# Work moved off GpSimd in an RWKV-7 mixer, a branch moved inside a layer of experts, and two weight loads swapped

## The chip, the cores and the metric

The kernel runs on one core of a Trainium2 chip. The metric is the device time of one execution, in microseconds (us). TensorE (PE) does the matrix products; VectorE (DVE), ScalarE (ACT) and GpSimd (POOL) do the element-wise work; SyncE (SP) issues nearly all DMA transfers. Each engine takes its own instructions in order and waits on semaphores for the others.

## The reference

256 tokens of width 1024, all in float32, pass through a first block (two layers of retention and block attention, not touched here) and a second block of two layers. Each layer of the second block is a mixer followed by a two-level mixture of 32 experts. The two mixers, cut to what matters:

```python
def even_mixer(h, ...):                    # layer 0
    u = h @ w_in
    m = u_rw + (token_shift(u_rw) - u_rw) * mu
    r, k, v, dw, da, dg = split(m)
    decay = exp(-exp(-softplus(-(w0 + tanh(dw) @ w2)) - 0.5))
    a = sigmoid(a0 + da @ a2);  g = sigmoid(dg) @ g2
    kk = heads(k * k_k)
    kk = kk / max(sqrt(sum(kk * kk, -1)), 1e-12)      # the norm of kk
    k = k * (1 + (a - 1) * k_a)
    y = rwkv7_recurrence(r, decay, k, v, -kk, kk * a) # S = S(diag w + a b^T) + v k^T ; y = S r
    bonus = sum(r * k * r_k, -1) * v
    o_rw = (groupnorm(y) * ln_g + ln_b + bonus) * g
    return concat([o_rw, multiscale_pool(u_pool)]) @ w_out

def odd_mixer(h, ...):                     # layer 1
    q, k, v, u_s5 = split(h @ w_in)
    o_attn = differential attention over q, k, v
    y = Re(C states) + D u_s5              # S5: one complex diagonal state per group
    z = gelu(y);  o_ssm = z * sigmoid(z @ w_glu)
    return concat([o_attn, o_ssm]) @ w_out
```

The experts (`hier_moe`) pick one of eight groups for a token and two of its four experts, and each expert is `down(silu(gate(x)) * up(x))`.

## The kernel before

**Weights.** A float32 product is made of three faster ones: the weight is split into a rounded part `hi` (a copy on ACT) and the rest `lo` (a subtraction, named `wlo`). Weights stand in a ring of SBUF slots `w0`, `w1`, ... `load_w` takes the next slot of a written-out order (`self.order`) and issues the load on SP's queue. The load waits there until the slot's last reader is done, and everything behind it in the queue waits as well.

**Even mixer** (`rwkv`, lines 1160 to 1530). The projections are made in pieces of 128 columns by `shifted` (PE at L1208 to L1210, 24 matmuls a piece from `hi` and `lo`), evacuated by DVE at L1213 and mixed with the token before by ACT at L1214 and DVE at L1215. The `lo` parts of the twelve pieces of k, r and v (four each, in this order) come from POOL at L1076; those of the pooling branch behind them come from DVE at L328. Then the decay's running sum (L1254), the norm of kk (an inverse square root by Newton's method, the chain `kkn` at L265 to L272 on tiles of 128x16, transposed by PE at L1280, spread by PE at L1289 and multiplied in at L1290), and block-diagonal operands `bbd`, `kbd`, `vbd` of two heads each (64 rows of one, 64 of the other). The recurrence is then solved in chunks of 64 tokens: products inside a chunk (L1403) and between chunks (L1411 to L1413), a small triangular inverse on DVE (L1421 to L1446, result `Tn`), and block products on PE (L1502). `LabO` and `LkO` hold the between-chunk products in block-diagonal form; DVE writes them at L1451 and L1482 as the PSUM tile times a 0/1 mask "bd". `P1` and `P2` are the gate and bonus of the output, made on POOL at L1334 to L1342.

**Experts** (`moe`). Eight groups of four experts, `for e0 in range(0, 32, 4)`. Each expert takes three matrices of 2 MB through the ring. An expert that more than 32 tokens chose is finished by `overflow`, a loop inside `tc.If(nblk > 0)`; with these inputs the branch (L1005) isn't taken, but every engine still passes it. It stands ahead of the last group, e0 = 28.

**Odd mixer** (`odd_heads`). SP's loads in their order: the matrices of q, k and S5's u, then `Tt`, S5's Toeplitz table (eight transfers at L1866 that read rows of 128 float32 from a DRAM scratch `s5H`), then v's matrix, the first half of `odd_w_out`, `s5_glu`, the second half. `Tt` is first read by the matmuls at L2041, v's matrix by the projection `ev`.

A scheduler sorts each engine's instructions by priority and by its own estimate of when they can start; `self.after(x)` puts what is issued inside it behind instruction x.

Of the kernel before, what the change touches and what calls it, by code (L numbers as in the profile page):

```python
# [19 lines left out]
T = 256  # L20
# [65 lines left out]
def even_consts():  # L86
    c = Packer()
    q = np.arange(128)
    h, s = q // 64, q % 64
    t = np.arange(64)  # L90
    same = lambda a, b, n: (a[:, None] // n) == (b[None, :] // n)
    lt = s[:, None] < t[None, :]
    both = lambda m: np.stack([m * (h[:, None] == g) for g in range(2)], axis=1)
    c.add("m16", lt & same(s, t, 16))
    c.add("incl", s[:, None] <= t[None, :])
    c.add("mo1", both(lt & same(s, t, 32) & ~same(s, t, 16)))
    c.add("mo2", both(lt & ~same(s, t, 32)))
    c.add("strict", both(lt))
    c.add("bd", both(np.ones((128, 64))))
    c.add("eye16", np.tile(np.eye(16).reshape(1, 256), (128, 1)))  # L100
    c.add("half", np.stack([q % 2 == 0, q % 2 == 1], axis=1))
    c.add("centre", (h[:, None] == h[None, :]) * (np.eye(128) - 1.0 / 64))
    sel = np.zeros((128, 4, 8))
    for p in range(4):
        sel[q, p, 2 * p + h] = 1.0
    c.add("sel", sel)
    selT = np.zeros((128, 4, 128))
    selT[:8] = sel.transpose(2, 1, 0)
    pm = np.zeros((128, 4, 3, 128))
# [37 lines left out]
class K:  # L147
# [112 lines left out]
    def rsqrt(self, sm, v, n, name, scratch=None):  # L260
        nc = self.nc
        if scratch is None:
            scratch = [sm.tile([128, n], F32, name=name + c) for c in ("_y", "_a", "_h")]
        y, a, h = scratch
        nc.vector.tensor_scalar(y.bitcast(I32), v.bitcast(I32), -0.5, float(0x5f3759df),  # L265
                                op0=ALU.mult, op1=ALU.add)
        for _ in range(2):
            nc.vector.tensor_mul(a, y, y)
            nc.vector.tensor_mul(h, a, v)
            nc.vector.tensor_scalar(a, h, 0.375, -1.25, op0=ALU.mult, op1=ALU.add)  # L270
            nc.vector.tensor_mul(a, a, h)
            nc.vector.scalar_tensor_tensor(y, a, 1.875, y, op0=ALU.add, op1=ALU.mult)  # L272
        return y
# [606 lines left out]
    def moe(self, l):  # L880
# [6 lines left out]
        with ctx:  # L887
# [11 lines left out]
            for e0 in range(0, 32, 4):  # L899
                last = e0 == 28  # L900
                if l == 0 and e0 == 8:
                    self.side = self.s5_prep()
                if e0 == 28:
                    if l == 0:
                        self.tick(99)
                    self.overflow(l, R, wk, pool, acc)
# [240 lines left out]
    def rwkv(self, keep):  # L1147
# [54 lines left out]
        def shifted(w, c, i, dst):  # L1202

            ps = X([128, T])
            wh, wl = w[c] if type(w) is list else self.wsplit(w, c, last_lo if i in (4, 5) and i not in (4, 5, 6, 7, 0, 1, 2, 3, 8, 9, 10, 11) else None,
                                                             nc.gpsimd if i in (4, 5, 6, 7, 0, 1, 2, 3, 8, 9, 10, 11) else None)
            for k in range(8):
# [54 lines left out]
        lam = Eg[:, :, 64:65].rearrange("p (a b) o -> p a (b o)", a=4)  # L1262
        for src, dst in ((0, 0), (1, 3), (2, 5)):
            nc.vector.tensor_copy(E6[:, :, dst], lam[:, :, src])
        nc.vector.tensor_mul(E6[:, :, 1], lam[:, :, 0], lam[:, :, 1])
        nc.vector.tensor_mul(E6[:, :, 4], lam[:, :, 1], lam[:, :, 2])
        nc.vector.tensor_mul(E6[:, :, 2], E6[:, :, 1], lam[:, :, 2])

# [3 lines left out]
        for p in range(4):  # L1272
            shifted(wr_, p, p, r[:, p])
        sv = prep.tile([128, 16], F32, name="kkv")
        for t in range(2):
            nc.vector.tensor_scalar(sv[:, 8 * t:8 * t + 8], ss[t], 1e-24, None, op0=ALU.max)
        rs_ = self.rsqrt(prep, sv, 16, "kkn")
        q = W([8, T])
        for t in range(2):
            nc.tensor.transpose(q[:, t * 128:(t + 1) * 128], rs_[:, 8 * t:8 * t + 8], self.ident)  # L1280
        rs = prep.tile([128, T], F32, name="kkr")[0:8]
        nc.vector.tensor_copy(rs, q)
        hka = prep.tile([128, 2, 4], F32, name="hka")
# [9 lines left out]
        u16 = lambda x: x.rearrange("p a (b t) -> p (a b) t", t=64)  # L1293
        nc.vector.tensor_mul(k, k, f)
        ar = AR0.rearrange("p a b x t -> p (a b) x t")
        nc.vector.scalar_tensor_tensor(ar[:, :, 0], u16(kk), -1.0, Eg[:, :, 0:64], op0=ALU.mult, op1=ALU.mult)
        nc.vector.tensor_scalar(ta, ta, 0.5, 0.5, op0=ALU.mult, op1=ALU.add)
        nc.vector.tensor_mul(kk, kk, ta)
        for h in range(2):
            hs = slice(64 * h, 64 * h + 64)  # L1300
            nc.vector.tensor_mul(bbd[hs, :, h], u16(kk)[hs], Ei[hs])
            nc.gpsimd.tensor_mul(kbd[hs, :, h], u16(k)[hs], Ei[hs])


        nc.vector.tensor_mul(ar[:, :, 1], u16(r), Eg[:, :, 1:65])

        rk = sq
        nc.gpsimd.tensor_mul(rk, r, k)
        srk = prep.tile([128, 32], F32, name="srk")
# [4 lines left out]
        for t in range(2):  # L1314
# [7 lines left out]
        wv_ = load(2)
        v = prep.tile([128, 4, T], F32, name="v", tag="tk")
        for p in range(4):
            shifted(wv_, p, 8 + p, v[:, p])
        for h in range(2):
            hs = slice(64 * h, 64 * h + 64)
            nc.scalar.activation(vbd[hs, :, h], u16(v)[hs], AF.Copy)
        for t in range(2):
# [3 lines left out]
            nc.scalar.activation(g, q, AF.Copy)  # L1333
            nc.gpsimd.tensor_mul(P1[:, t], g, lngb[:, 0])  # L1334
            q = W([128, 4, 128])
            for p in range(4):
# [3 lines left out]
                                 bon[:, t][:, :, None].to_broadcast([128, 8, 64]))  # L1340
            nc.gpsimd.tensor_add(P2[:, t], P2[:, t], lngb[:, 1])
            nc.gpsimd.tensor_mul(P2[:, t], P2[:, t], g)  # L1342

# [104 lines left out]
        for p in range(4):  # L1448
            qa, qb = offd(p, bbd, X if p in (0, 1, 2, 3) else W)
            for j, q in enumerate((qa, qb)):  # L1450
                nc.vector.tensor_mul(LabO[:, p, 3 * j:3 * j + 3], b4(q[:, :, 0:64], 3), mk("bd", 3))  # L1451
            cp = lambda o, n, x: nc.scalar.activation(
# [16 lines left out]
        for p in range(4):  # L1469
# [11 lines left out]
            for j, q in enumerate((qa, qb)):  # L1481
                nc.vector.tensor_mul(LkO[:, 3 * j:3 * j + 3], b4(q[:, :, 0:64], 3), mk("bd", 3))  # L1482
            cp = lambda o, n, x: nc.scalar.activation(
# [357 lines left out]
    def odd_heads(self, sm, pa, m, ctx):  # L1841
# [4 lines left out]
        load = lambda b, **kw: self.load_w(A["odd_in"][b], (8, 512), **kw)  # L1846
        self.order = [0, 4, 0, 4, 0, 2, 4, 3]
        wq = load(0, parts=2)
# [12 lines left out]
        wk_, wu = load(1), load(3)  # L1861
        Vt, Wt = (S[n_].rearrange("p (g x) -> p g x", g=32) for n_ in ("V", "W"))
        Tt = self.load_slot()
        for k in range(8):
            src = bass.AP(tensor=S["H"].tensor, offset=S["H"].offset + 16 * k, ap=[[240, 16], [32 * 240, 32], [1, 128]])
            nc.sync.dma_start(Tt[16 * k:16 * k + 16].rearrange("p (g x) -> p g x", g=32), src)  # L1866
        Tt = Tt.rearrange("p (g x) -> p g x", g=32)
        wv = load(2)
        wo0 = self.load_w(A["odd_w_out"][0], (8, 512))
        wgl = self.load_w(A["s5_glu"], (4, 512))  # L1870
        wo1 = self.load_w(A["odd_w_out"][1], (8, 512))
# [403 lines left out]
```

## Time and profile before

| | |
|---|---|
| median of 3 runs | 1618.96 us (1616.09 to 1620.35) |
| the profiled execution | 1615.62 us, of which the span of its instructions is 1613.6 us |
| PE busy | 1304.4 us (81%), mean granted clock 0.91 |
| DVE, ACT, POOL busy | 629.3, 406.5, 256.0 us |
| DMA | 499.22 MB, 309 GB/s in the mean |

By place in the trace: the first block ends at about 345 us, the even mixer at 565, the first layer of experts at 1017, the odd mixer at 1165, and the second layer of experts runs to the end. Busy times are to be read with care: PE's is the sum of its matmuls at whatever clock it was granted, so a stretch at half clock shows more of it for the same work.

### The profile page before, as it was taken

The page shows a single profiled execution, that of the slowest core. Times are in us where ns is not written, and L with a number is a line of the kernel's source. Part 1 is how long each engine was busy: PE and PEld are TensorE (multiplying, and loading weights), DVE is VectorE, ACT ScalarE, POOL GpSimd, SP SyncE. Part 2 cuts the span into 40 slices and gives each one's busy share as a digit, 9 for nine tenths or more (in the row PEclk, how much of TensorE's full clock was granted, in tenths as well). Part 3 has the DMA queues.
Part 4 walks back from the last instruction along what each step waited for, and adds up shares of the span by engine and source line. Part 5 has one row for each costly group of instructions (what it writes and reads, how often), then busy time and mean ns, then how long its engine had stood idle before and what let it go on. Part 6 is the DMA issues. An engine that isn't in the chain of part 4 may idle for free. (4 is left out here: it accounts for less than half of the span.)

```text
span 1613.6 us, 31866 instructions
## 1 busy us (share of the span) xinstructions
PE 1304.4 (81%) x13994; PEld 959.8 (59%) x13994; DVE 629.3 (39%) x1460; ACT 406.5 (25%) x759; POOL 256.0 (16%) x322
## 2 busy tenths in 40 slices
PE   7999999986989788678686658877888677777767
PEld 6887788785879665535544425656765533443434
DVE  7687678768583611511111001738611111010011
ACT  5455545554332200001110001525300000000001
POOL 2200020045323100271452000202300000000000
PEclk9999999997899799779898979987999988898879
DMA  9554344332242889999999999558799999999996
GB/s 352 196 190 157 128 185 179 133 147 105 95 157 101 317 361 425 402 426 425 420 419 422 424 381 416 158 94 326 297 425 425 424 426 426 426 426 426 424 423 287
DMA packets 51368, 499.22 MB, mean 309 GB/s; under 512 B 9452, under 2 KB 16784, under 8 KB 20632
## 3 DMA queue, kind: packets, MB, share of 16 engines
q1 hardware_dynamic: 50648, 492.40, 75.9%
q0 software_dynamic: 288, 4.19, 0.7%
q8 instruction: 113, 1.85, 0.5%
q10 hardware_dynamic: 288, 0.52, 0.1%
q14 instruction: 31, 0.25, 0.0%
HBM read 495.06 MB, written 2.04 MB: 308 GB/s over the span
## 5 line engine op out<-in xcount | busy, mean ns | idle before, releaser
L856 PE MATMUL mm<-w,xt 128*32 128x128 f32 x8192 | 300.3, 299 | 109.1 <-DMA w<-in_moe_w_up_dram 41.3
L856 PEld LDWEIGHTS mm<-w,xt 128*32 128x32 f32 x8192 | 254.2, 120 | 150.8 <-issue 89.2
L936 PE MATMUL mm<-w,hidT 128*32 128x512 f32 x896 | 189.8, 667 | 53.0 <-DMA w<-in_moe_w_down_dram 52.9
L328 DVE TENSOR_TENSOR wlo<-w,whi 128x1024 fp32r<-128x1024 f32 x116 | 143.1, 1239 | 55.3 <-ACT whi L327 54.5
L327 ACT ACTIVATE whi<-w 128x1024 fp32r<-128x1024 f32 x124 | 130.7, 1058 | 130.9 <-PE pj L338 89.0
L860 DVE SCALAR_TENSOR_TENSOR hid<-hid,mm 128x128 f32<-128x128 f32 x64 | 18.3, 286 | 371.5 <-ACT hid L859 371.5
L936 PEld LDWEIGHTS mm<-w,hidT 128*32 128x32 f32 x896 | 43.2, 118 | 166.2 <-issue 121.7
L336 PE MATMUL pj<-whi,hT 128*128 128x512 f32 x316 | 123.4, 404 | 19.1 <-ACT whi L327 17.5
L337 PE MATMUL pj<-wlo,hT 128*128 128x512 f32 x316 | 126.0, 403 | 0.0
L338 PE MATMUL pj<-whi,hT 128*128 128x512 f32 x316 | 122.9, 397 | 0.7 <-DVE hT L308 0.7
L870 DVE SCALAR_TENSOR_TENSOR y<-mm,slotsc,y 128x512 fp32r<-128x512 f32 x36 | 26.9, 750 | 190.2 <-ACT y L869 187.5
L845 PEld LDWEIGHTS tp<-ohs,x 128*128 128x128 f32 x512 | 73.8, 232 | 30.2 <-issue 25.1
L845 PE MATMUL tp<-ohs,x 128*128 128x128 f32 x512 | 77.2, 319 | 17.9 <-DVE ohs L797 17.4
L869 ACT ACTIVATE y<-mm,slotsc 128x512 fp32r<-128x512 f32 x36 | 24.7, 687 | 261.5 <-PE mm L936 239.5
L859 ACT ACTIVATE hid<-mm 128x128 f32<-128x128 f32 x64 | 17.7, 277 | 271.8 <-PE mm L856 271.8
L336 PEld LDWEIGHTS pj<-whi,hT 128*128 128x128 f32 x316 | 60.3, 192 | 32.6 <-ACT whi L327 17.7
L337 PEld LDWEIGHTS pj<-wlo,hT 128*128 128x128 f32 x316 | 60.3, 191 | 13.8 <-DVE wlo L328 1.4
L338 PEld LDWEIGHTS pj<-whi,hT 128*128 128x128 f32 x316 | 60.0, 190 | 13.3 <-DVE hT L308 1.1
L877 PE MATMUL acc<-y,ohT 128*128 128x512 f32 x144 | 49.4, 444 | 12.3 <-ACT y L869 6.2
L846 DVE TENSOR_TENSOR xt<-tp,pk 128x512 f32<-128x512 f32 x32 | 22.1, 691 | 91.0 <-PE tp L845 91.0
L864 ACT ACTIVATE hidT<-tp 128x128 f32<-128x128 f32 x64 | 17.7, 277 | 142.4 <-PE tp L863 142.4
L877 PEld LDWEIGHTS acc<-y,ohT 128*128 128x128 f32 x144 | 23.2, 193 | 42.2 <-issue 17.1
(728 smaller groups left out, 2128.3 us busy)
## 6 DMA issues: line engine op xcount, KB each, us to landing
w<-in_moe_w_gate_dram SPq DMA_DIRECT2D x64, 2048.0 KB, 30.1
w<-in_moe_w_up_dram SPq DMA_DIRECT2D x64, 2048.0 KB, 21.1
w<-in_moe_w_down_dram SPq DMA_DIRECT2D x54, 2048.0 KB, 28.8
w<-in_w_in_dram SPq DMA_DIRECT2D x14, 2048.0 KB, 7.7
w<-in_moe_w_down_dram SPq DMA_DIRECT2D x16, 1024.0 KB, 15.8
w<-in_w_out_dram SPq DMA_DIRECT2D x4, 2048.0 KB, 7.8
w<-in_w_ple_gate_dram SPq DMA_DIRECT2D x4, 2048.0 KB, 7.6
w<-in_even_in_dram SPq DMA_DIRECT2D x4, 2048.0 KB, 7.8
```

The source lines that it names most:

```text
L327: nc.scalar.activation(h, w[:, i:i + s], AF.Copy)
L328: (engine or nc.vector).tensor_sub(l, w[:, i:i + s], h.bitcast(F32))
L336: nc.tensor.matmul(out, ah, wh, start=start, stop=False)
L337: nc.tensor.matmul(out, ah, wl, start=False, stop=False)
L338: return nc.tensor.matmul(out, al, wh, start=False, stop=stop)
L845: nc.tensor.matmul(p[:, k], xk[t][:, 4 * h + k], ohs[:, t], start=t == 0, stop=t == 1)
L846: nc.vector.tensor_mul(xt[:, ks], p, R["g"][:, ks, None].to_broadcast([128, 4, 128]))
L856: nc.tensor.matmul(gu[32 * q:32 * q + 32, i], xt(k), w[:, k, 128 * q:128 * q + 128], start=k == 0, stop=k == 7)
L869: nc.scalar.activation(y[0][b][r], dn[r], AF.Copy, scale=sc[r, 0:1])
L870: nc.vector.scalar_tensor_tensor(y[1][b][r], dn[r], sc[r, 0:1], y[0][b][r].bitcast(F32), op0=ALU.mult, op1=ALU.subtract)
L877: self.nc.tensor.matmul(acc[t][b], ohT[r, t], y[i][b][r], start=start and i == 0, stop=stop and i == 1)
L936: nc.tensor.matmul(dn[32 * j:32 * j + 32], hT[j][:, k], wd[j][:, 4 * b + k], start=k == 0, stop=k == 3)
```

## The change

In the even mixer the twelve `lo` subtractions of L1076, `kbd`, `rk` (tile `sq`), `P1` and `P2` move from POOL to DVE, so that no element-wise product of the projections is left on POOL; the kkn chain gets a higher priority and some products are put behind it with `after`; v's load and projection come ahead of the bonus. The masks of `LabO` and `LkO` become a zero fill on POOL and two half-tile copies on ACT (`heads`). The overflow branch moves from e0 = 28 to e0 = 16. In the odd mixer v's matrix is loaded ahead of `Tt`, into `Tt`'s old slot 4 (`Tt` takes slot 0, v's old one), and `s5_glu` ahead of the first half of `odd_w_out`.

```diff
-                if e0 == 28:
-                    if l == 0:
-                        self.tick(99)
+                if l == 0 and last:
+                    self.tick(99)
+                if e0 == 16:
                     self.overflow(l, R, wk, pool, acc)
...
-    def wsplit(self, w, c, behind=None, engine=None):
+    def wsplit(self, w, c):
...
-        with self.after(behind) if behind else ExitStack():
-            (engine or nc.vector).tensor_sub(wl, wc, wh.bitcast(F32))
+        nc.vector.tensor_sub(wl, wc, wh.bitcast(F32))
...
+        with self.tc.high_priority(offset=300):
+            sv = prep.tile([128, 16], F32, name="kkv")
+            for t in range(2):
+                nc.vector.tensor_scalar(sv[:, 8 * t:8 * t + 8], ss[t], 1e-24, None, op0=ALU.max)
+            rs_ = self.rsqrt(prep, sv, 16, "kkn")
+            kkn = self.last_rs
...
+        with self.after(kkn):
+            for src, dst in ((0, 0), (1, 3), (2, 5)):
+                nc.vector.tensor_copy(E6[:, :, dst], lam[:, :, src])
...
-            nc.gpsimd.tensor_mul(kbd[hs, :, h], u16(k)[hs], Ei[hs])
+            with self.after(kkr):
+                nc.vector.tensor_mul(kbd[hs, :, h], u16(k)[hs], Ei[hs])
...
+        wv_ = load(2)
+        v = prep.tile([128, 4, T], F32, name="v", tag="tk")
+        for p in range(4):
+            with self.after(kkr):
+                shifted(wv_, p, 8 + p, v[:, p])
+
         rk = sq
-        nc.gpsimd.tensor_mul(rk, r, k)
+        nc.vector.tensor_mul(rk, r, k)
...
-            nc.gpsimd.tensor_mul(P1[:, t], g, lngb[:, 0])
+            nc.vector.tensor_mul(P1[:, t], q, lngb[:, 0])
...
-            nc.gpsimd.tensor_add(P2[:, t], P2[:, t], lngb[:, 1])
-            nc.gpsimd.tensor_mul(P2[:, t], P2[:, t], g)
+            nc.vector.tensor_add(P2[:, t], P2[:, t], lngb[:, 1])
+            nc.vector.tensor_mul(P2[:, t], P2[:, t], g)
...
+        for z in (LabO, *LkOs):
+            nc.gpsimd.memset(z, 0.0)
+
+        def heads(dst, q):
+
+            for h in range(2):
+                hs = slice(64 * h, 64 * h + 64)
+                nc.scalar.activation(dst[hs, :, h], q[hs, :, 0:64], AF.Copy)
...
-                nc.vector.tensor_mul(LabO[:, p, 3 * j:3 * j + 3], b4(q[:, :, 0:64], 3), mk("bd", 3))
+                heads(LabO[:, p, 3 * j:3 * j + 3], q)
...
-        self.order = [0, 4, 0, 4, 0, 2, 4, 3]
+        self.order = [0, 4, 0, 4, 0, 4, 2, 3]
...
+        wv = load(2)
         Tt = self.load_slot()
...
-        wv = load(2)
+        wgl = self.load_w(A["s5_glu"], (4, 512))
         wo0 = self.load_w(A["odd_w_out"][0], (8, 512))
-        wgl = self.load_w(A["s5_glu"], (4, 512))
         wo1 = self.load_w(A["odd_w_out"][1], (8, 512))
```

How this changes an engine's order is shown at three places. First DVE in the even mixer, around the kkn chain (`kkn_y`, `kkn_a`, `kkn_h` are its tiles, `kkv` its input; `up`, `r` the evacuation and mixing of a piece of r). Before:

```order
L265 TENSOR_SCALAR kkn_y<-kkv 128x16
L1264 COPY E_2924<-Eg 128x4 x3
L1265 TENSOR_TENSOR E_2924<-Eg 128x4
L1266 TENSOR_TENSOR E_2924<-Eg 128x4
L268 TENSOR_TENSOR kkn_a<-kkn_y 128x16
L1215 SCALAR_TENSOR_TENSOR r<-up_3015,evc,r 128x256
L1267 TENSOR_TENSOR E_2924<-E_2924,Eg 128x4
L1294 TENSOR_TENSOR k<-k,sq 128x1024
L269 TENSOR_TENSOR kkn_h<-kkn_a,kkv 128x16
L1297 TENSOR_SCALAR ta<-ta 128x1024
L1213 TENSOR_TENSOR up_3016<-x,rstdb 128x256
L270 TENSOR_SCALAR kkn_a<-kkn_h 128x16
```

After:

```order
L264 TENSOR_SCALAR kkn_y<-kkv 128x16
L1212 SCALAR_TENSOR_TENSOR r<-up_3015,evc,r 128x256
L267 TENSOR_TENSOR kkn_a<-kkn_y 128x16
L268 TENSOR_TENSOR kkn_h<-kkn_a,kkv 128x16
L269 TENSOR_SCALAR kkn_a<-kkn_h 128x16
L1210 TENSOR_TENSOR up_3016<-x,rstdb 128x256
L270 TENSOR_TENSOR kkn_a<-kkn_a,kkn_h 128x16
L271 SCALAR_TENSOR_TENSOR kkn_y<-kkn_a,kkn_y 128x16
L267 TENSOR_TENSOR kkn_a<-kkn_y 128x16
L268 TENSOR_TENSOR kkn_h<-kkn_a,kkv 128x16
L269 TENSOR_SCALAR kkn_a<-kkn_h 128x16
L1212 SCALAR_TENSOR_TENSOR r<-up_3016,evc,r 128x256
```

The products of `E`, k and ta (`L1264` to `L1267`, `L1294`, `L1297`) no longer stand inside the chain; only the evacuations of r do.

Second POOL in the same mixer, from its first work on the projections on. Before:

```order
L1076 TENSOR_TENSOR wlo<-w_2939,whi 128x1024 x2
L1165 MEMSET bbd 128x2048
L1165 MEMSET kbd 128x2048
L1165 MEMSET vbd 128x2048
L679 MEMSET pk 128x2x4
L1176 COPY sel<-evc 128x32
L1076 TENSOR_TENSOR wlo<-w_2939,whi 128x1024 x2
L1076 TENSOR_TENSOR wlo<-w_3274,whi 128x1024 x4
L1076 TENSOR_TENSOR wlo<-w_3474,whi 128x1024
L1302 TENSOR_TENSOR kbd<-k,G 64x16x64 x2
L1076 TENSOR_TENSOR wlo<-w_3474,whi 128x1024 x3
L1308 TENSOR_TENSOR sq<-r,k 128x1024
```

After:

```order
L1163 MEMSET bbd 128x2048
L1163 MEMSET kbd 128x2048
L1163 MEMSET vbd 128x2048
L678 MEMSET pk 128x2x4
L1174 COPY sel<-evc 128x32
L1403 MEMSET lko_3756 128x768
L1440 COPY ux<-evc 128x256
L1403 MEMSET early 128x768
L1525 TENSOR_TENSOR u_3753<-Lr,evc 128x512 x2
L1403 MEMSET LabO 128x3072
L1449 MEMSET Tt 128x2048
L1449 MEMSET Tn 128x2048
```

Up to the products of `u` nothing is left there but fills and two small copies; the three new fills stand ahead of those of Tt and Tn.

Third SP's queue in the odd mixer. Before:

```order
L246 DMA w_8662<-in_odd_in_dram 128x4096
L1866 DMA w_8664<-s5H 16x32x128 x8
L246 DMA w_8673<-in_odd_in_dram 128x4096
L246 DMA w_8675<-in_odd_w_out_dram 128x4096
L246 DMA w_8677<-in_s_glu_dram 128x2048
```

After:

```order
L245 DMA w_8681<-in_odd_in_dram 128x4096
L245 DMA w_8683<-in_odd_in_dram 128x4096
L1878 DMA w_8685<-s5H 16x32x128 x8
L245 DMA w_8694<-in_s_glu_dram 128x2048
L245 DMA w_8696<-in_odd_w_out_dram 128x4096
```

v's matrix passes the eight transfers of the table, and `s5_glu` passes `odd_w_out`.

## Rows read from the trace of the kernel before

**Rows 1.** The page, the span in 40 slices: what the DMA engines moved.
```profile
GB/s 352 196 190 157 128 185 179 133 147 105 95 157 101 317 361 425 402 426 425 420 419 422 424 381 416 158 94 326 297 425 425 424 426 426 426 426 426 424 423 287
```

**Rows 2.** Windows: us, busy of PE, PEld, DVE, ACT, POOL, PEclk, DMA share, GB/s.
```profile
340.00:360.00 20.00, 15.88 (x117) 15.25 (x116) 12.31 (x35) 10.57 (x18) 14.54 (x9) 0.91 0.26 97
360.00:380.00 20.00, 14.54 (x89) 12.54 (x88) 15.40 (x23) 10.53 (x23) 10.34 (x5) 0.77 0.57 211
380.00:400.00 20.00, 11.81 (x96) 11.60 (x94) 18.45 (x29) 7.34 (x9) 13.89 (x6) 0.84 0.00 0
400.00:420.00 20.00, 18.12 (x106) 16.41 (x107) 15.32 (x25) 4.17 (x6) 3.21 (x2) 0.71 0.28 106
420.00:440.00 20.00, 20.00 (x118) 16.83 (x118) 9.83 (x9) 7.89 (x13) 9.25 (x7) 1.00 0.29 106
```

**Rows 3.** Timeline of PE there: start, us, instruction, idle before and its releaser.
```profile
373.03 1.22 PE L1244 MATMUL x<-lr,w 64*128 64x256 f32 x2 [5.46 <-DVE up L1213]
401.37 0.59 PE L1280 MATMUL w<-pk,kkn_y 128*8 128x128 f32 x2 [9.56 <-DVE kkn_y L272]
480.94 2.47 PE L1502 MATMUL w<-Tn,u 128*128 128x128 f32 x10 [5.47 <-DVE Tn L1446]
```

**Rows 4.** Timeline of DVE there.
```profile
367.63 4.75 DVE L1215 SCALAR_TENSOR_TENSOR k<-up,evc,k 128x256 f32<-128x256 f32 x2 [0.96 <-ACT k L1214]
373.88 0.49 DVE L1215 SCALAR_TENSOR_TENSOR k<-up,evc,k 128x256 f32<-128x256 f32 x1 [0.32 <-ACT k L1214]
391.44 2.23 DVE L272 SCALAR_TENSOR_TENSOR kkn_y<-kkn_a,kkn_y 128x16 f32<-128x16 f32 x1
401.14 0.17 DVE L272 SCALAR_TENSOR_TENSOR kkn_y<-kkn_a,kkn_y 128x16 f32<-128x16 f32 x1
```

**Rows 5.** Timeline of POOL there.
```profile
367.27 4.83 POOL L1076 TENSOR_TENSOR wlo<-w,whi 128x1024 fp32r<-128x1024 f32 x2 [1.76 <-ACT whi L1074]
388.35 5.28 POOL L1302 TENSOR_TENSOR kbd<-k,G 64x1024 f32<-64x1024 f32 x2 [2.43 <-DVE kkn_h L269]
```

**Rows 6.** Groups by line, shapes apart, 340 to 500 us: busy us, mean ns, idle before.
```profile
L638 DVE SCALAR_TENSOR_TENSOR e<-rotu,e 128x512 f32<-128x512 f32 x2 | 5.1, 2532 | 1.1 <-ACT rotu L636 1.1
...
L328 DVE TENSOR_TENSOR wlo<-w,whi 128x1024 fp32r<-128x1024 f32 x4 | 4.9, 1223 | 1.5 <-ACT whi L327 1.5
...
L1451 DVE TENSOR_TENSOR LabO<-x,evc 128x384 f32<-128x384 f32 x8 | 4.0, 547 | 0.0
...
L1215 DVE SCALAR_TENSOR_TENSOR lr<-up,evc,lr 128x256 f32<-128x256 f32 x2 | 3.5, 1766 | 1.1 <-ACT lr L1214 1.1
...
L1452 ACT ACTIVATE ArbT<-x 128x192 f32<-128x192 f32 x4 | 1.3, 330 | 2.8 <-DVE LabO L1451 2.6
```

**Rows 7.** The branch's line: min/median/max ns, first and last start.
```profile
L1005 PEldq COMPARE_BRANCH  x2: 6432/6454/6477, 958.2 to 1552.7; - x2
```

**Rows 8.** Timeline of PE behind the branch in layer 0.
```profile
965.80 6.53 PE L845 MATMUL tp<-ohs,x 128*128 128x128 f32 x32 [7.46 <-DVE ohs L797]
```

**Rows 9.** Windows: behind the branch in layer 0, and the end of layer 1.
```profile
960.00:970.00 10.00, 4.20 (x20) 4.23 (x21) 1.26 (x3) 0.00 (x0) 0.00 (x0) 0.56 0.72 261
...
1595.00:1600.00 5.00, 4.14 (x105) 3.21 (x106) 0.57 (x2) 0.55 (x2) 0.00 (x0) 1.00 0.52 211
```

**Rows 10.** Timeline of SP in the odd mixer.
```profile
1041.92 9.17 SPq L1866 DMA_DIRECT2D w<-s5H  x8
1052.02 1.40 SPq L246 DMA_DIRECT2D w<-in_odd_in_dram  x1
```

**Rows 11.** Window of the odd mixer while the table is on its way.
```profile
1040.00:1060.00 20.00, 20.00 (x160) 16.18 (x161) 15.60 (x44) 10.01 (x15) 0.00 (x0) 1.00 1.06 95
```

**Rows 12.** Timeline of the odd mixer on ACT and PE, and PE's first read of the table.
```profile
1070.24 2.95 ACT L327 ACTIVATE whi<-w 128x1024 fp32r<-128x1024 f32 x3 [10.00 <-DMA w<-in_odd_in_dram]
1071.35 1.22 PE L336 MATMUL pj<-whi,hT 128*128 128x512 f32 x2 [8.52 <-ACT whi L327]
...
1087.29 0.62 PE L2041 MATMUL at<-w,U 128*32 128x128 f32 x16
```

More of the change, by code (lines that the diff above doesn't have):

```diff
@@ L98, in even_consts @@
     c.add("strict", both(lt))
-    c.add("bd", both(np.ones((128, 64))))
     c.add("eye16", np.tile(np.eye(16).reshape(1, 256), (128, 1)))
@@ L271, in rsqrt @@
             nc.vector.tensor_mul(a, a, h)
-            nc.vector.scalar_tensor_tensor(y, a, 1.875, y, op0=ALU.add, op1=ALU.mult)
+            self.last_rs = nc.vector.scalar_tensor_tensor(y, a, 1.875, y, op0=ALU.add, op1=ALU.mult)
         return y
@@ L1204, in shifted @@
             ps = X([128, T])
-            wh, wl = w[c] if type(w) is list else self.wsplit(w, c, last_lo if i in (4, 5) and i not in (4, 5, 6, 7, 0, 1, 2, 3, 8, 9, 10, 11) else None,
-                                                             nc.gpsimd if i in (4, 5, 6, 7, 0, 1, 2, 3, 8, 9, 10, 11) else None)
+            wh, wl = w[c] if type(w) is list else self.wsplit(w, c)
             for k in range(8):
@@ L1262, in rwkv @@
         lam = Eg[:, :, 64:65].rearrange("p (a b) o -> p a (b o)", a=4)
[L1263 to L1267, printed above, removed]
+        with self.after(kkn):
+            for src, dst in ((0, 0), (1, 3), (2, 5)):
+                nc.vector.tensor_copy(E6[:, :, dst], lam[:, :, src])
+            nc.vector.tensor_mul(E6[:, :, 1], lam[:, :, 0], lam[:, :, 1])
+            nc.vector.tensor_mul(E6[:, :, 4], lam[:, :, 1], lam[:, :, 2])
+            nc.vector.tensor_mul(E6[:, :, 2], E6[:, :, 1], lam[:, :, 2])
         wr_ = load(1)
@@ L1273, in rwkv @@
             shifted(wr_, p, p, r[:, p])
[L1274 to L1277, printed above, removed]
         q = W([8, T])
@@ L1281, in rwkv @@
         rs = prep.tile([128, T], F32, name="kkr")[0:8]
-        nc.vector.tensor_copy(rs, q)
+        kkr = nc.vector.tensor_copy(rs, q)
         hka = prep.tile([128, 2, 4], F32, name="hka")
@@ L1293, in rwkv @@
         u16 = lambda x: x.rearrange("p a (b t) -> p (a b) t", t=64)
-        nc.vector.tensor_mul(k, k, f)
+        with self.after(kkn):
+            nc.vector.tensor_mul(k, k, f)
         ar = AR0.rearrange("p a b x t -> p (a b) x t")
         nc.vector.scalar_tensor_tensor(ar[:, :, 0], u16(kk), -1.0, Eg[:, :, 0:64], op0=ALU.mult, op1=ALU.mult)
-        nc.vector.tensor_scalar(ta, ta, 0.5, 0.5, op0=ALU.mult, op1=ALU.add)
+        with self.after(kkn):
+            nc.vector.tensor_scalar(ta, ta, 0.5, 0.5, op0=ALU.mult, op1=ALU.add)
         nc.vector.tensor_mul(kk, kk, ta)
@@ L1319, in rwkv @@
             nc.vector.tensor_copy(bon[:, t], q)
[L1322 to L1325, printed above, removed]
         for h in range(2):
@@ L1481, in rwkv @@
             for j, q in enumerate((qa, qb)):
-                nc.vector.tensor_mul(LkO[:, 3 * j:3 * j + 3], b4(q[:, :, 0:64], 3), mk("bd", 3))
+                heads(LkO[:, 3 * j:3 * j + 3], q)
             cp = lambda o, n, x: nc.scalar.activation(
```

## The prediction

> **What bounds the kernel now.** I read the page's slices first [rows 1]; one slice is 1613.6/40 = 40.3 us. From slice 15 to 24 (565 to 970 us) and from 30 to the end the DMA engines move 400 to 426 GB/s: the two layers of experts are bound by their weights. In slices 9 to 13 (about 360 to 520 us) they move 95 to 157, so the even mixer is bound by the engines, and so is the odd mixer (slices 25 to 28 hold it, 94 to 326). A microsecond saved in a mixer starts the stream of experts behind it a microsecond earlier, and the stream's length stays.
>
> Then the windows of the even mixer [rows 2]. PE's busy time there is mostly work, but at a granted clock of 0.91, 0.77, 0.84, 0.71 and 1.00. Busy time by clock is PE's work at full clock: 14.5 + 11.2 + 9.9 + 12.9 + 20.0 = 68.4 us in 100. The missing 31.6 us are idle PE and the low clock behind each idle stretch. The waits of PE say who: 5.46 us on DVE's evacuations and 9.56 us on the kkn chain [rows 3]. DVE is not slow by itself there. Two mixings of k took 4.75 us beside two subtractions of POOL that took 4.83; one such took 0.49 later. A step of kkn on 128x16 numbers took 2.23 us beside POOL's `kbd`, the last one 0.17 [rows 4, 5]. Five of the steps from 389 to 401 us are as long as that one. So a two-input operation of POOL holds DVE, tiny operations too, and the longest wait of PE is one made of such holds.
>
> **The change, part by part.** Threshold for a difference that can be told: 0.3%, 4.9 us.
>
> *A. POOL out of the projections, kkn together.* DVE's load in 340 to 440 us is 12.31 + 15.40 + 18.45 + 15.32 + 9.83 = 71.3 us [rows 2]. What goes, by rows 4 and 6: k 4.75 - 2 x 0.49 = 3.8; five kkn steps of 2.23 - 0.17, 10.3; lr 3.5 - 2 x 0.49 = 2.5; L638's two of 512 columns 5.1 - 1.2 = 3.9 (0.6 each, half of a subtraction of 1024 columns at 1.22). Together 20.5. What comes: twelve subtractions at 1.223, 14.7; `kbd` 2.4 and `rk` 1.2 as three operations of 1024 columns; P1 and P2 six of 512 columns, 3.7. Together 22.0. DVE then has 72.8 us to do, PE 68.4. The mixer to 440 us could thus lose 27 us at most by DVE and 31.6 by PE. It won't lose all: the first `lo` of v now stands behind kkr and `kbd` on DVE (2.4 + 1.2 us, of which I count 2 on PE's path), those of the pooling branch behind AR and the products (3 us), and one more idle stretch means one more stretch of low clock (5 us, as 400 to 420 us lost 7.1 now). 31.6 - 2 - 3 - 5 = 21.6, and I take 20: 80 us with DVE 91% busy. From below: if none of DVE's long operations gets shorter, 71.3 + 22.0 = 93.3 us of DVE, and the gain is 7 at most and may be nothing. **A: -20, bounds -27 and 0.**
>
> *B. Masks.* Sixteen DVE products of 0.55 us go (eight of L1451 [rows 6], eight like them at L1482), 8.8 us. ACT gets 32 copies of half the rows; a copy of 128x192 takes 0.33 us there [rows 6], so 10.6 us in some 50 us in which ACT is mostly free. The last wait on this path is PE's 5.47 us for `Tn` [rows 3], a DVE result; only L1451's eight (4.4 us) stand ahead of it. The three zero fills (128x4608 in all) have no row; a POOL product of 1024 columns takes 2.4 us [rows 5], so 10.9 us at most, and POOL has little else by then. Were they late, ACT's copies of LabO and PE behind them would wait for up to 3 x 2.4 = 7.2 us. I take -2, nearer to the DVE row, because part of the 4.4 us lies beside PE's work. **B: -2, bounds -4.4 and +7.**
>
> *C. The branch in e0 = 16.* PE spends 6.45 us in the branch in either layer [rows 7], then waits 7.46 us for DVE's masks that no engine could begin ahead of it, and gathers for 6.53 us [rows 8]: 14 us in which no expert's matrix is used up. In layer 0 the DMA engines dropped to 261 GB/s for 10 us [rows 9], (425 - 261)/425 x 10 = 3.9 us of the stream. In layer 1 the last loads came at 211 GB/s for 5 us [rows 9], 2.5 us, because PE ran late at the end. In mid layer SP has issued four loads of the group ahead of the branch as before, so the hole of layer 0 moves and stays; behind it three groups follow in which PE catches up, so that the end of both layers runs with PE on time. I take 0 for the hole and -2 for the end of layer 1. Bounds: -6.4 (both), and +14 if PE's 14 us empties the queue in a place where it did not before. **C: -2.**
>
> *D. v's matrix ahead of the table.* ACT idled 10.00 us for v's matrix and PE 8.52 us behind it [rows 12]. The matrix was issued at 1052.02, behind the table's eight issues of 9.17 us [rows 10], and then lay behind the table's bytes: the engines were busy all the time (share 1.06) at 95 GB/s [rows 11], 1.9 MB in 20 us of the table's 2 MB. The Trainium skill (DMA: Bandwidth & Descriptors, Specifications) gives 512 bytes as enough for line rate; the table's pieces are 128 float32, just that. By it, an estimate of 2 MB at the 425 GB/s of the experts' stream, the table would pass in about 5 us, v's matrix would have come in time, and D would be worth nothing: a sum of -24. The trace disagrees, with 95 GB/s. Now the matrix is issued at 1041.92, when slot 4 is free, and comes long before PE wants it at 1062.8 (1071.35 - 8.52). The table waits for slot 0, free by 1052.02 at the latest, so it comes some 10 us later. Issued at 1041.92, at 95 to 105 GB/s, it needs about 22 us; issued at 1052.02, it is there at 1074. PE reads it first at 1087.29 [rows 12], then 8.5 us earlier: 1078.8. It is just hidden, by 5 us; a table that takes 27 us starts to cost. `s5_glu` now waits for slot 4, free when v's matrix is split, long ahead of its use. Behind this the chain to the experts keeps its order. I take 8 of the 8.5 us; the low clock behind the gap could add 3. **D: -8, bounds -11 and 0.**
>
> Sum: -20 - 2 - 2 - 8 = -32, against the profiled execution's 1615.62: 1583.6. The median of the runs lies 0.2% (3.3 us) above that execution, so 1587 us.
>
> **Rivals.**
>
> *DVE becomes the bound.* PE now waits for each of twelve `lo` parts on an engine that in 380 to 400 us was busy 18.45 of 20 us [rows 2]. For it: DVE's 72.8 us must fit in 80 with its own waits for PE and ACT in between. Against: 20.5 us of the load that made it full go. If A gives 5 and B nothing: -15, so 1604.
>
> *The table is late.* PE's matmuls at L2041 then wait in order, and the gap moves from `ev` to them. For it: 5 us of room only. Then D is 0: 1595. If v's matrix and the table share the engines the table needs longer still.
>
> *The branch opens new holes.* In mid layer the queue is at its fullest use; 14 us of PE at rest in each layer, of which 10 fall on the stream: C is +20 and the time 1609. For it: the 261 GB/s of layer 0. Against: in layer 1 the ring has more free slots, as no S5 tables stand in it, and three groups follow in either layer in which PE, faster than the stream, catches up.
>
> *The clock, which ends on the other side.* PE in the even mixer is fed piece by piece by DVE; if the small waits between pieces keep the granted clock at its lower level (0.5, 1.2 GHz) from 340 to 440 us, the 68.4 us of work take 137 instead of 100, +37, and with B, C and D the sum is +25: 1644. It costs more than all else gives once 0.63 of that work runs at the low level (68.4 x 1.63 = 111.5, against 100 + 12). Against: where PE idles only now and then (420 to 440 us) the clock was 1.00 [rows 2], and the low windows are those with idle of 5 us and more.
>
> **How the numbers follow.** Forecast 0.62 (its own range 1577 to 1597); DVE the bound 0.18; table late 0.08; branch 0.07, of which 0.03 at half its price together with a DVE that is the bound (-15 + 12 = -3, no change); clock 0.05. The range 1574 to 1608 holds the forecast with the lower bounds of A and D part way, the first two rivals and half of the third. Faster by over 0.3% (below 1614): 0.92; within: 0.03; slower: 0.05, the clock.
>
> **What would show it.** A: the kkn steps at 0.17 us each in a row, the 9.56 us wait of PE gone, windows of the mixer at a clock near 0.9 or over, the first L1403 products some 20 us earlier. B: ACT busier by 10 us, `Tn`'s wait not longer. C: the drop to 261 GB/s at e0 = 16 of layer 0 (about 750 us) and none near its end. D: the 8.52 us gone, SP's table issue near 10 us behind v's, no wait at the table's matmuls. I would be wrong if PE's waits name DVE's `lo` parts, if the low clock stays with the idle gone, or if a shorter mixer leaves the start of the experts' stream where it was.

## The result: 2.4% faster, and the profile after

The changed kernel takes 1579.61 us in the median of 4 runs (1578.68 to 1580.19), before 1618.47 (1616.09 to 1620.35): a ratio of 0.976 (0.9743 to 0.9777), 38.9 us. The prediction was 1587 in a range of 1574 to 1608. Its profiled execution has a span of 1578.1 us, 35.5 less than before.

Where the span got shorter is read from four places that both traces have. PE begins the counting products of the first router (L763, before L764), behind the even mixer, at 533.30 us, before 558.68: 25.4 us earlier. It begins the odd mixer at 989.90, before 1018.70: 28.8 earlier, so 3.4 more. It begins those of the second router at 1127.06, before 1163.83: 36.8 earlier, 8.0 more. The end is 35.5 earlier, so layer 1 gave 1.3 back. Another profile of the same kernel (the control below, span 1576.4) has these four at 531.17, 987.89, 1125.58 and the end. The first differs by 2.1 us, the steps from one place to the next by at most 0.6.

The executions don't all enter the even mixer at the same time. By the row of eight transposes (`x<-pk,x`) with which PE begins it, the stretches are these (us):

| | begin | even mixer | layer 0 | odd mixer | layer 1 |
|---|---|---|---|---|---|
| before | 340.81 | 217.9 | 460.0 | 145.1 | 449.8 |
| changed | 341.62 | 191.7 | 456.6 | 137.2 | 451.0 |
| control | 340.16 | 191.0 | 456.7 | 137.7 | 450.8 |

So the even mixer got 26.2 us shorter and not 25.4; the untouched first block ended 0.8 later in the changed kernel's profile. In eight profiles in which the even mixer is as in the changed kernel it takes 190.9 to 191.7 us, which makes its length the sharpest measure for the runs on A and B below.

The windows of the even mixer, which answer to [rows 2] (us, busy PE, PEld, DVE, ACT, POOL, PEclk, DMA share, GB/s):

```profile
340.00:360.00 20.00, 18.43 (x144) 17.43 (x143) 15.34 (x42) 12.26 (x20) 5.56 (x5) 1.00 0.49 176
360.00:380.00 20.00, 18.16 (x146) 16.98 (x145) 18.07 (x53) 15.22 (x29) 0.00 (x0) 1.00 0.38 145
380.00:400.00 20.00, 18.18 (x132) 17.15 (x131) 19.41 (x27) 6.78 (x9) 0.00 (x0) 0.91 0.29 106
400.00:420.00 20.00, 20.00 (x115) 16.80 (x115) 15.21 (x22) 7.96 (x15) 3.29 (x5) 1.00 0.30 106
420.00:440.00 20.00, 19.71 (x136) 17.19 (x135) 14.85 (x61) 14.59 (x49) 7.65 (x4) 1.00 0.54 211
```

By busy time and clock as in the prediction, PE now does 18.4 + 18.2 + 16.5 + 20.0 + 19.7 = 92.8 us of full-clock work in these 100 us, where it did 68.4: 24.4 us more. The clock fell below 1.00 in one window only. DVE is at 19.41 of 20 us between 380 and 400, and the longest wait of PE for it from 340 to 440 us is 1.20 us, for a `lo` part (below).

The waits of PE at the places of [rows 3], and the first read of the table (PE's timeline):

```profile
365.08 0.48 PE L1241 MATMUL x<-lr,w 64*128 64x256 f32 x1 [1.51 <-ACT lr L1234]
...
381.61 0.38 PE L1280 MATMUL w<-pk,kkn_y 128*8 128x128 f32 x2
...
386.23 0.58 PE L1206 MATMUL x<-hT,wlo 128*128 128x256 f32 x1 [1.20 <-DVE wlo L1074]
...
464.17 2.00 PE L1513 MATMUL w<-Tn,u 128*128 128x128 f32 x8 [1.66 <-POOL u L1525]
...
1044.96 0.62 PE L2052 MATMUL at<-w,U 128*32 128x128 f32 x16
```

5.46 us became 1.51. The wait for `kkn_y` (9.56) is gone: its transposes (L1280) begin without idle. Of `Tn`'s 5.47 us, 1.66 are left, now for POOL's `u`. The table's first matmul has no wait either.

The groups by line of the same DVE operations as in [rows 4, 6], 330 to 480 us (busy us, mean ns, idle before):

```profile
L637 DVE SCALAR_TENSOR_TENSOR e<-rotu,e 128x512 f32<-128x512 f32 x4 | 2.7, 686 | 0.8 <-ACT rotu L635 0.8
...
L1212 DVE SCALAR_TENSOR_TENSOR k<-up,evc,k 128x256 f32<-128x256 f32 x4 | 1.8, 482 | 0.7 <-ACT k L1211 0.7
...
L1212 DVE SCALAR_TENSOR_TENSOR lr<-up,evc,lr 128x256 f32<-128x256 f32 x2 | 0.9, 478 | 0.0
...
L271 DVE SCALAR_TENSOR_TENSOR kkn_y<-kkn_a,kkn_y 128x16 f32<-128x16 f32 x2 | 0.4, 176 | 0.1
```

Mixing a piece of k went from up to 2.4 us to 0.48, lr's from 1.77 to 0.48, L638 (now L637) from 2.53 to 0.69, kkn's steps to 0.18.

Windows around the branch in layer 0, where it now stands (it is passed at 747 us), which answer to [rows 9]:

```profile
740.00:750.00 10.00, 7.35 (x40) 2.48 (x35) 1.50 (x2) 1.37 (x2) 0.29 (x1) 0.96 1.04 412
750.00:760.00 10.00, 5.15 (x34) 5.18 (x34) 1.97 (x6) 0.00 (x0) 4.82 (x9) 0.66 0.94 371
```

The hole moved and shrank: 371 GB/s for 10 us where it was 261, (425 - 371)/425 x 10 = 1.3 us of the stream against 3.9. SP's queue in the odd mixer, for [rows 10]:

```profile
1012.85 0.33 SPq L245 DMA_DIRECT2D w<-in_odd_in_dram  x1
1022.97 8.90 SPq L1878 DMA_DIRECT2D w<-s5H  x8
1042.50 0.35 SPq L245 DMA_DIRECT2D w<-in_s_glu_dram  x1
1045.21 0.35 SPq L245 DMA_DIRECT2D w<-in_odd_w_out_dram  x1
```

The first row is v's matrix, 10.1 us ahead of the table. And the window while the table is on its way, for [rows 11]:

```profile
1030.00:1040.00 10.00, 10.00 (x110) 7.76 (x102) 1.63 (x2) 2.61 (x6) 0.00 (x0) 1.00 1.26 107
```

The DMA engines are still busy all the time at 107 GB/s, but PE is at 10 of 10 us beside the table. By windows of 1 us the rate falls between 1042 and 1043 us, some 2 to 3 us ahead of the table's first read.

### The profile page after: what moved, and what is told of

Same layout as the page of the kernel before. It is cut to its first block, busy times and chain, and to the rows that moved or that the text cites. A ratio compares the mean times of both kernels' runs of the same rounds, so it can differ in the third digit from the quotient of the medians.

```text
span 1578.1 us, 31896 instructions
## 1 busy us (share of the span) xinstructions
PE 1287.3 (82%) x13994; PEld 944.5 (60%) x13994; DVE 617.6 (39%) x1465; ACT 416.0 (26%) x791; POOL 214.1 (14%) x304
## 5 line engine op out<-in xcount | busy, mean ns | idle before, releaser
L935 PE MATMUL mm<-w,hidT 128*32 128x512 f32 x896 | 185.5, 653 | 48.5 <-DMA w<-in_moe_w_down_dram 48.0
L869 DVE SCALAR_TENSOR_TENSOR y<-mm,slotsc,y 128x512 fp32r<-128x512 f32 x36 | 26.9, 750 | 190.0 <-ACT y L868 187.3
L844 PEld LDWEIGHTS tp<-ohs,x 128*128 128x128 f32 x512 | 67.9, 217 | 30.4 <-issue 22.5
L844 PE MATMUL tp<-ohs,x 128*128 128x128 f32 x512 | 70.8, 304 | 17.6 <-DVE ohs L796 17.6
L335 PEld LDWEIGHTS pj<-whi,hT 128*128 128x128 f32 x316 | 59.8, 190 | 24.4 <-ACT whi L326 9.2
L862 PE MATMUL tp<-pk,hid 128*128 128x128 f32 x64 | 22.3, 349 | 30.7 <-DVE hid L860 30.2
```

The source lines that it names most:

```text
L335: nc.tensor.matmul(out, ah, wh, start=start, stop=False)
L844: nc.tensor.matmul(p[:, k], xk[t][:, 4 * h + k], ohs[:, t], start=t == 0, stop=t == 1)
L862: nc.tensor.transpose(p, hid, self.ident)
L869: nc.vector.scalar_tensor_tensor(y[1][b][r], dn[r], sc[r, 0:1], y[0][b][r].bitcast(F32), op0=ALU.mult, op1=ALU.subtract)
L935: nc.tensor.matmul(dn[32 * j:32 * j + 32], hT[j][:, k], wd[j][:, 4 * b + k], start=k == 0, stop=k == 3)
```

## The experiments

Each is the changed kernel with one thing different; ratios are to the kernel before, run beside it on the same chip. One per cent is 16.2 us.

**The changed kernel again**, as a control.

> The changed kernel itself, for comparison with the others of this group: 1579 to 1581.

1578.84 us (1578.40 to 1581.17), ratio 0.9764 (0.9751 to 0.9777). The two results of this kernel together, 0.9762, are what the runs below are compared with; differences of less than about 0.15% (2.4 us) lie within their intervals.

**POOL takes its work back; order kept.** `kbd` stands here for all of it: the twelve subtractions of `wsplit`, `rk`, `P1` and `P2` go back in the same way.

```diff
-                nc.vector.tensor_mul(kbd[hs, :, h], u16(k)[hs], Ei[hs])
+                nc.gpsimd.tensor_mul(kbd[hs, :, h], u16(k)[hs], Ei[hs])
```

> The changed kernel with every operation that was moved to DVE back on POOL (twelve subtractions, kbd, rk, P1, P2); the order of the kkn chain and v's place stay. The run without the kkn order cost 11 us, so the place of the chain counts. If POOL's holds count as well, as the long DVE operations of before say (20.5 us of them), DVE's steps of kkn are long again and the time is 1592 to 1602. The rival, that the order is all: 1579 to 1584, since DVE has 22 us less to do.

1595.05 us, ratio 0.986 (0.9845 to 0.9875): 0.0098, 15.8 us slower than with the work on DVE. The even mixer takes 205.8 us, in the control 191.0. Its DVE groups, 340 to 420 us:

```profile
L1212 DVE SCALAR_TENSOR_TENSOR k<-up,evc,k 128x256 f32<-128x256 f32 x4 | 5.7, 1450 | 1.3 <-ACT k L1211 1.3
...
L271 DVE SCALAR_TENSOR_TENSOR kkn_y<-kkn_a,kkn_y 128x16 f32<-128x16 f32 x2 | 2.6, 1295 | 0.1
```

and PE's wait at L1241 in its timeline:

```profile
373.84 1.22 PE L1241 MATMUL x<-lr,w 64*128 64x256 f32 x2 [5.47 <-DVE up L1210]
```

For k these are the numbers of before to the tenth (its mixing 5.7 us there too, PE's wait 5.46). The kkn chain is another matter, and my expectation that its steps would be long again was wrong: of its eleven operations one is held (2.42 us, which with one of 0.17 makes the mean of 1295 ns above), the chain lasts 5.0 us from first start to last end where it lasted 15.3, and PE's wait at the transposes is gone, with the work back on POOL. What is left there is a shorter wait for the copy `kkr` behind it, which stands on DVE behind other products and a mixing of r of 1.57 us (PE's timeline):

```profile
392.62 0.38 PE L1280 MATMUL w<-pk,kkn_y 128*8 128x128 f32 x2
397.73 3.78 PE L1289 MATMUL x<-kkr,selT 8*128 8x256 f32 x8 [4.72 <-DVE kkr L1282]
```

`kbd`, beside which the steps of before were held, now stands behind `kkr`, so the order keeps the two apart. POOL's holds count, but outside the chain: besides k, the mixing of lr (3.5 us, in the changed kernel 0.9) and L637 (5.1 and 1.4) are as long as before. None of PE's waits from 340 to 440 us names POOL, so it is not that POOL makes its results too slowly for PE.

**The kkn chain without priority and constraints; POOL still out.** Every `after(kkn)` and `after(kkr)` goes as the one shown.

```diff
-        with self.tc.high_priority(offset=300):
+        with ExitStack():
             sv = prep.tile([128, 16], F32, name="kkv")
...
-        with self.after(kkn):
+        with ExitStack():
```

> The changed kernel without the priority and the order constraints of the kkn chain (POOL still out of the projections, v's load and code still ahead of the bonus). My theory, that POOL's holds made the chain long and not its place: its steps stay at 0.17 us, the products that come between cost 2 to 4 us: 1581 to 1584. The rival, that the order of the chain was what PE's 9.56 us were made of: 1587 to 1590.

1591.09 us, ratio 0.9826 (0.9812 to 0.9839): 0.0064, 10.4 us slower; the even mixer takes 201.1 us. The rival was right here, and my expectation of 2 to 4 us fell. PE waits at the transposes of kkn again, for almost as long as before (PE's timeline, then DVE's):

```profile
391.09 0.59 PE L1280 MATMUL w<-pk,kkn_y 128*8 128x128 f32 x2 [9.15 <-DVE kkn_y L271]
```

```profile
379.39 0.17 DVE L267 TENSOR_TENSOR kkn_a<-kkn_y 128x16 f32<-128x16 f32 x1
379.47 1.23 DVE L1074 TENSOR_TENSOR wlo<-w,whi 128x1024 fp32r<-128x1024 f32 x1
380.61 2.46 DVE L1305 TENSOR_TENSOR kbd<-k,G 64x1024 f32<-64x1024 f32 x2
383.09 0.43 DVE L1210 TENSOR_TENSOR up<-x,rstdb 128x256 f32<-128x256 f32 x1
383.44 0.17 DVE L268 TENSOR_TENSOR kkn_h<-kkn_a,kkv 128x16 f32<-128x16 f32 x1
383.52 1.22 DVE L1074 TENSOR_TENSOR wlo<-w,whi 128x1024 fp32r<-128x1024 f32 x1
```

No step is held; each is 0.17 us. But what POOL did now stands between the steps on DVE: two small steps of the chain lie 4 us apart. For this wait, moving the work alone would have turned the hold into a queue; the run before shows that the order alone takes the wait away.

**Added POOL products nobody reads**, twelve of 128x768 on two SBUF operands. `dump` is a tile of their own, `hi_i` the rounding copy of the piece.

```diff
+            if type(w) is not list:
+                with self.after(self.hi_i):
+                    nc.gpsimd.tensor_mul(dump, cst[:, 0:768], cst[:, 0:768])
```

> The changed kernel with twelve added POOL products of 128x768, each of two operands in SBUF, one behind the rounding of each piece of k, r and v; nobody reads the results. Theory of the hold: DVE operations beside them grow by part of some 1.8 us each, 12 to 20 us in all, of which PE feels 5 to 15: 1585 to 1595. The rival, that DVE's long operations of before came from waiting for POOL's results and not from POOL being busy: no change, 1579 to 1581.

1588.17 us, ratio 0.9816 (0.9802 to 0.9829): 0.0054, 8.7 us slower by the medians; the profile shows the slowest of its five executions (1592.56), whose even mixer takes 203.6 us. No instruction waits for these products, so it is POOL being busy that costs. They ran in one piece, 348.8 to 371.9 us. DVE's groups at 349 to 372 us, in the control and then with the products:

```profile
L269 DVE TENSOR_SCALAR rsxa<-rsxh 128x2 f32<-128x2 f32 x2 | 0.3, 166 | 0.0
L271 DVE SCALAR_TENSOR_TENSOR rstd<-rsxa,rstd 128x2 f32<-128x2 f32 x2 | 0.3, 160 | 0.1
```

```profile
L269 DVE TENSOR_SCALAR rsxa<-rsxh 128x2 f32<-128x2 f32 x2 | 2.9, 1436 | 0.0
L271 DVE SCALAR_TENSOR_TENSOR rstd<-rsxa,rstd 128x2 f32<-128x2 f32 x2 | 2.6, 1315 | 0.1
```

**Added POOL fills**, three zero fills of 128x768 in place of each product.

```diff
-                    nc.gpsimd.tensor_mul(dump, cst[:, 0:768], cst[:, 0:768])
+                    for _ in range(3):
+                        nc.gpsimd.memset(dump, 0.0)
```

> The same with three zero fills of 128x768 for each product, about as much POOL time, with nothing read. If a hold needs POOL to read SBUF, no change: 1579 to 1582. If any busy POOL holds DVE, as with the products: 1585 to 1595.

1582.19 us, ratio 0.9778 (0.9765 to 0.9792): 0.0016, 2.6 us slower, at the edge of what can be told and neither of the two outcomes expected. The even mixer takes 194.0 us, 2.3 to 3.1 more than in the changed kernel. The trace says why it lies between. DVE's groups at 349 to 372 us, in the control and then beside the fills:

```profile
L1212 DVE SCALAR_TENSOR_TENSOR k<-up,evc,k 128x256 f32<-128x256 f32 x4 | 1.8, 482 | 0.7 <-ACT k L1211 0.7
L1225 DVE TENSOR_SCALAR kk<-k,evc 128x256 f32<-128x256 f32 x4 | 1.4, 348 | 0.0
```

```profile
L1230 DVE TENSOR_SCALAR kk<-k,evc 128x256 f32<-128x256 f32 x4 | 3.1, 768 | 0.0
...
L1217 DVE SCALAR_TENSOR_TENSOR k<-up,evc,k 128x256 f32<-128x256 f32 x4 | 1.8, 472 | 0.1
```

Beside a fill the operations with two tensors from SBUF keep their time (482 and 472 ns), and the ones with a single tensor wait (348 to 768). Beside a product both kinds wait, though not each operation: L270's two, with two tensors, kept 0.16 us in that run.

**The masks back on DVE**, for `LkO` as shown for `LabO`; the zero fills go and the constant "bd" comes back.

```diff
-                heads(LabO[:, p, 3 * j:3 * j + 3], q)
+                nc.vector.tensor_mul(LabO[:, p, 3 * j:3 * j + 3], b4(q[:, :, 0:64], 3), mk("bd", 3))
```

> The changed kernel with the 16 mask products back on DVE (no zero fills, no half copies on ACT). My theory: 4.4 of the 8.8 us stand ahead of the triangular inverse and part of them lies beside PE's work: +2 us, 1581 to 1583. The rival: with the POOL work now on DVE that engine sets the pace, and the 8.8 us come whole: 1587 to 1589.

1583.88 us, ratio 0.9777 (0.976 to 0.9793): 0.0015, 2.4 us slower; the size fits the forecast, at the edge of the intervals. The even mixer takes 193.8 us, 2.1 to 2.8 more than in the changed kernel. (Layer 0 and the odd mixer, where nothing differs, are 1.2 and 1.6 us longer than in the control as well; why stays open.) PE's wait for `Tn` is 2.59 us in it (by DVE), against 1.66 (by POOL).

**The odd mixer's loads in the old order.**

```diff
-        self.order = [0, 4, 0, 4, 0, 4, 2, 3]
+        self.order = [0, 4, 0, 4, 0, 2, 4, 3]
...
-        wv = load(2)
         Tt = self.load_slot()
...
+        wv = load(2)
+        wo0 = self.load_w(A["odd_w_out"][0], (8, 512))
         wgl = self.load_w(A["s5_glu"], (4, 512))
-        wo0 = self.load_w(A["odd_w_out"][0], (8, 512))
```

> The changed kernel with the odd mixer's loads in the old order (table ahead of v's matrix, old slots). My theory: the 8.5 us wait of PE for v's matrix is back and passes whole to the end: 1587 to 1589. The rival, that the experts' stream or the softmax behind it absorbs part of the gap: 1582 to 1585.

1585.56 us, ratio 0.9795 (0.9782 to 0.9808): 0.0033, 5.3 us slower, between the two expectations. The wait is back (PE's timeline):

```profile
1040.41 1.22 PE L335 MATMUL pj<-whi,hT 128*128 128x512 f32 x2 [8.32 <-ACT whi L326]
```

From the start of the odd mixer to the second router it takes 1133.89 - 986.76 = 147.1 us, in the control 1125.58 - 987.89 = 137.7: the swap saves 9.4 us there. From the router to the end it takes 1583.9 - 1133.89 = 450.0, in the control 1576.4 - 1125.58 = 450.8: 0.8 us are given back. The other profiles agree: layer 1 takes 449.8 and 450.0 us in the two with the old order of loads, 450.6 to 451.1 in the eleven with the new one and a branch.

**The branch**, in other places and left out. First ahead of the last group again:

```diff
-                if l == 0 and last:
-                    self.tick(99)
-                if e0 == 16:
+                if e0 == 28:
+                    if l == 0:
+                        self.tick(99)
                     self.overflow(l, R, wk, pool, acc)
```

> The changed kernel with the overflow branch back ahead of the last group (e0 = 28), all else as changed. My reading of the two traces: the move gains 3.4 us by the end of layer 0 and loses 1.3 us in layer 1, so putting it back costs about 2 us: 1581 to 1583 against 1579.6. The rival: the 3.4 us of layer 0 come from the earlier start of its stream and not from the branch, then 1579 to 1580, or less by what layer 1 loses now.

1584.72 us (1581.62 to 1586.60), ratio 0.9791 (0.9777 to 0.9805). It was run again:

> The changed kernel with the branch back at e0 = 28 in both layers, once more, since the first time scattered (1581.6 to 1586.6) and had no run of the changed kernel beside it. By the traces +2 us, 1580 to 1583; the rival, that the position costs nothing: 1578 to 1580.

1583.35 us, ratio 0.9795 (0.9778 to 0.9813). Both lie 0.003 above the changed kernel, 4.7 and 5.3 us; by the spans of the profiles (1579.7 and 1579.4, against 1578.1 and 1576.4) it is 2.3. But both profiles with the branch at 28 are of the fastest of their five executions, so no trace shows what the slower ones lose. Layer 0, from first router to odd mixer, takes 990.84 - 532.55 = 458.3 and 459.0 us with the branch at 28, and 456.6 and 456.7 in the two profiles of the changed kernel. In all ten profiles with the branch at 16 or 4 it takes 456.4 to 458.1, so the difference is clear of that spread by little. With e0 == 28 for layer 1 alone:

> The changed kernel with the branch at e0 = 16 in layer 0 and at e0 = 28 in layer 1. If, as the two traces read, the move gains 3.4 us in layer 0 and loses 1.3 in layer 1: 1577 to 1579. The rival, that layer 1 gains by the move too and lost its 1.3 us elsewhere (its prefetch): 1580 to 1583.

1579.27 us, ratio 0.9771 (0.9754 to 0.9788): as the changed kernel. Layer 1 takes 450.6 us in it, 451.0 and 450.8 in the changed kernel: its branch may stand in either place. With e0 == 4 in both:

> The changed kernel with the branch at e0 = 4 in both layers. There S5's tables don't yet stand in layer 0's ring, and SP issues all eight gate and up loads of the group ahead of the branch, so the hole in layer 0 goes: 1577 to 1579, near the kernel without a branch. The rival, that early in a layer PE has not yet got ahead of the stream and 14 us of rest cost more: 1581 to 1590.

1580.03 us, ratio 0.9769 (0.9752 to 0.9785), layer 0 in 456.6 us: no different from e0 = 16, neither better by the eight loads ahead of it nor worse by its early place. Without branch and loop:

> The changed kernel without the overflow branch and its loop in either layer (no expert overflows with these inputs, so the work left out is only the loop that isn't entered). What the branch still costs where it stands now: by the windows of the changed kernel a hole of 1.3 us in the stream of layer 0 (371 GB/s for 10 us) and none in layer 1, so 1577 to 1579. The rival, that PE's 14 us at rest cost more than the stream shows: 1570 to 1575.

1577.98 us, ratio 0.9757 (0.9741 to 0.9774), layer 0 in 455.6 us and layer 1 in 449.5. The branch costs 1.0 and 1.5 us by these two lengths where it stands now, which is no more than the lengths scatter, and the ratio can't tell it from nothing. No experiment beat the changed kernel by more than the runs can tell.

## Why the prediction was right, point by point

**What bounds the kernel** held: the mixers' gains went through to the end. The first router came 25.4 us earlier, and layer 0 behind it took no longer.

**The sum** forecast 32 us, 22 of them in the even mixer, 0 in layer 0, 8 in the odd mixer and 2 in layer 1. Between the two traces these are 26.2, 3.4, 8.0 and -1.3, and -0.8 in the first block: 35.5. So the sum for the profiled execution, 1583.6, was 3.4 us too high (1580.19 measured). The other 3.9 us of the miss come from the step to the median: 3.3 us were added because the median of before lay that far above its profiled execution, but in the changed kernel the profiled execution was the slowest of the four and the median lies 0.6 below it. That offset was scatter.

**A** had the right mechanism and was sized too small. With B it was forecast at 22 us and measured 26.2 by the length of the even mixer (26.9 in the control's profile). The step that was off is the subtraction from 31.6: I took off 2 for v's first `lo`, 3 for those of the pooling branch and 5 for one more stretch of low clock. The windows after show 7.2 us missing in 100 in place of 31.6, a gain of 24.4, and the clock at 0.91 in one window. DVE did carry its load, at 19.41 of 20 us where it was fullest. That the work has to leave POOL is shown by the added products and by the work put back (8.7 and 15.8 us). But the step that made PE's 9.56 us out of five long kkn steps was wrong: with the order and POOL's work in its old place the wait is gone, and with the steps at 0.17 us but without the order it is 9.15. The order removes that wait, and I had costed it at nothing. The two parts add up more than they depend on each other: by the even mixer's length, against the control, the work put back costs 14.8 us, the order taken out 10.1 and the masks 2.8, together 27.6, and the mixer got 26.9 shorter.

**B** forecast 2 us; the run with the masks back is 2.4 us slower by the ratio, at the edge of its interval, and 2.1 to 2.8 by the even mixer's length. PE's last wait for `Tn` names POOL's `u` (1.66 us) and no fill.

**C** forecast 2 us, all of it at the end of layer 1, with the hole of layer 0 only moved. That the sum was near is luck, as the places were wrong. (The reading was off in one point too: the 6.45 us of the branch lie inside the 7.46 us that PE idles, from 958.3 to 965.8, and not ahead of them; the 14 us are 7.46 and 6.53.) The gain is in layer 0 (1.7 to 2.4 us by its length, 3.4 between the first two traces; the hole 1.3 us and not 3.9), and layer 1 doesn't care: with the new order of loads it takes 450.6 to 451.1 us with the branch at 16 and at 28. The 211 GB/s at its end, which the move was to mend, come there after the change too: 205 GB/s from 1559.5 to 1564.5 us, as far from the end. By the medians the whole move is worth 4.7 to 5.3 us, by the spans 2.3; which is nearer stays open.

**D** forecast 8 us. In the odd mixer it is 8.0 between the first two traces, and 9.4 from the run with the old order. The granted clock of the 10 us behind the gap was 0.63 before and 0.61 in that run; the control has no gap and 1.00 from 1020 to 1060 us. At the end 5.3 us by the ratios, 7.5 by the spans of two profiles. About 0.8 us is given back in layer 1; the rest of the difference lies within the intervals. The table came in time, by 2 to 3 us and not by 5. The row of 95 GB/s was the right one to go by, and not the estimate of 5 us for the table's bytes: the table moved at 107 GB/s after the change too. What limits it no run here shows; each of its eight transfers has pieces of 512 bytes and also writes 16 partitions only, and the two were not taken apart.

**The rivals.** DVE nearly is the bound (19.41 of 20 us), but PE waited for only one of its `lo` parts, 1.20 us; the clock rose; the table wasn't late; the branch opened no new hole. None of them came.

## What to carry to other kernels

Where small VectorE operations take ten times their usual time, look at what GpSimd does in the same microseconds before anything else; the work may be cheaper on the busier engine. Then look at what it displaces there: a latency chain on that engine must be put ahead of the new work, or PE waits for the queue as long as it did for the hold (9.15 us here, 9.56 before). And in one queue, put the load that is needed first ahead of one that the trace shows to be slow (107 GB/s here, where the experts' matrices move at 425), whatever its byte count says.

## What was not expected of the hardware

A GpSimd zero fill and a GpSimd product don't disturb VectorE alike. Beside fills, two-tensor operations kept 0.47 to 0.48 us and single-tensor ones went from 0.35 to 0.77, about the 0.74 us of one fill; beside products operations of both kinds went from 0.16 to 1.3 or 1.4. The Trainium skill (SBUF — State Buffer, section "SBUF: two separate sides") states this: the port pair that VectorE and GpSimd share is an exclusive lock, which a VectorE operation needs in a two-port mode, or with two SBUF inputs, and the latter only against a GpSimd operation that reads SBUF. The traces here agree with the split by kind in both runs. Which mode the single-tensor operations ran in is not seen in a trace.
